# Value projections with 512 moving columns in a decoder trunk's two mixers

## The chip, the core and the metric

The kernel runs on one core of a Trainium2 chip. The metric is the device time of one execution in microseconds (us); the time before is 1752.04, the median of 3 runs that lie between 1751.99 and 1752.09. Engines are named as in the profile: PE (TensorE, matmuls; PEld its weight loads), DVE (VectorE), ACT (ScalarE), POOL (GpSimd), SP (SyncE, which issues most DMA transfers).

## What is computed

A decoder trunk over 512 tokens with 1024 features, in float32: two layers, each a feed-forward block (half step), a mixer, and another feed-forward block (half step), each behind an RMS norm. The mixer of layer 0 is a gated linear attention, that of layer 1 a stick-breaking attention, called the softmax mixer here. Cut to the mixers:

```python
# layer 0: gated linear attention, 4 heads, keys of 128, values of 256
proj = h @ w_in                       # q 512, k 512, v 1024, g 1024, gate rank 16
q, k, v, g, gk_lr = split(proj)
log_a = log_sigmoid(gk_lr @ w_gk2 + b_gk) / 16
...                                   # decayed causal attention of each head: o
o = rmsnorm(o, o_norm) * silu(g)
y = o @ w_out

# layer 1: stick-breaking attention, 16 heads of 64
q, k, v = split(h @ w_in)             # 1024 each
z = q @ k.T / 8                       # strictly causal
w = exp(log_sigmoid(z) - reversed_cumsum(softplus(z)))
y = (w @ v) @ w_out
```

The feed-forward blocks are SwiGLU with 2816 hidden features.

## The kernel before

Every large product is taken in three matmuls: each float32 operand is split into a high part (rounded to fp32r, by an ACT cast) and a low part (the difference, by DVE), and high x high, high x low and low x high are summed in PSUM. For a weight block of 128 x 1024 the cast is line 152 (`wh`) and the difference line 153 (`wl`). Four pairs of such weight buffers exist (`bufs=4`), and two for the raw blocks as they arrive from memory (`raw`, `bufs=2`).

The projections of all phases stand in one queue, `Feed`. An entry has units (weight blocks to be cast) and a body, a generator that emits its matmuls in half-steps. `Feed.start` (lines 160 to 178) begins an entry: it casts the units of up to three entries as long as no more than four weight buffers are taken, and loads the raw blocks of up to six. The mixers' own work, head by head, draws from this queue: `step` takes two half-steps, `halves` single ones. A scheduler then orders the instructions of each engine by its own estimates; engines run their instructions in that order.

Two kinds of entries matter here. `feat` (line 218) has the weights stationary and 512 tokens moving, 24 matmuls with 512 columns in four half-steps; queries, keys and gates are made so. `tok` (line 238) has the tokens stationary, 128 at a time, and 256 weight columns moving: 4 token tiles x 8 blocks of 128 features x 3 = 96 matmuls with 256 columns in eight half-steps, in the PSUM tile `ps_t`. Values are made so, 256 columns an entry, two weight buffers each, and copied out by `evac_v` (lines 1069 and 1425).

Linear attention (`GLA`) queues 8 `feat` entries for queries and keys, then four `tok` entries (all values), then 8 `feat` entries for gates (lines 1042 to 1048). Its run (line 1350) goes over four heads. For each, `levels` prepares scores (`e`, `ps_S`), and `output` of the head before it makes decayed keys (`kd`, transposed by PE into `ps_kd`), states (`st`, `ps_s`) and outputs (`ps_o`, `ps_on`), with a `step` between the pieces (lines 1373 to 1397).

The softmax mixer (`SB`) queues pairs of `feat` entries (`pair(p)`: query and key of heads 2p and 2p+1) and four `tok` entries (`vals`) among them (lines 1421 and 1422). Its run (line 1559) takes 12 half-steps ahead of the heads (4 at line 1583, 8 at line 1587), and then 17 rounds. Round s emits head s's logits (`ps_z`), sigmoids on ACT, scans (`l`, line 1509) and products (`r`, line 1517) on DVE, and head s-1's transposes of `r` (`ps_T`, line 1531), copies (`wt`, line 1534) and, after every second head, the product with the values (`ps_oT`) and its split (`oh`, `ol`). The list `steps` (line 1589) says how many half-steps are drawn in each round. Each finished projection is scaled into `n` and split for the logits (`mq`, `kh`, `kl`, lines 1430 to 1471), at once before the heads, later at set points of a round.

Of the kernel before, what the change touches and what calls it, by code (L numbers as in the profile page):

```python
# [14 lines left out]
AF = mybir.ActivationFunctionType  # L15
# [3 lines left out]
P = 128  # L19
T = 512  # L20
D = 1024
KD = D // P
FF = 2816
NT = T // P
# [6 lines left out]
def turns(t):  # L31

    return t.rearrange("p (two n) -> p n two", two=2)


def flat(ps):

    return ps.rearrange("p (n two) -> p two n", two=2)


def pair(t):

    return t.rearrange("p (two n) -> p two n", two=2)
# [3 lines left out]
def decoder(ctx: ExitStack, tc: tile.TileContext, a: dict, out: bass.AP):  # L47
# [66 lines left out]
    class Entry:  # L114
# [4 lines left out]
        def __init__(self, units, body):  # L119
            self.units, self.body, self.W, self.views = units, body, None, None  # L120
            self.v = None
            self.open, self.sums_behind, self.casts_behind = True, None, None
            self.half = False

        def view(self):

# [5 lines left out]
        def split(self, after=None):  # L132
            if self.W is None:
                self.W = []
                for r, (_, _, n, m) in zip(self.view(), self.units):
# [20 lines left out]
    class Feed:  # L156
# [3 lines left out]
        def start(self):  # L160
            i = self.pos
            self.pos += 1
            used, v = 0, self.q[i].v or {}
            for e in self.q[i : i + 3]:
                if not e.open or e.v is not None and "copied" not in e.v:
                    break
                used += sum(n * m >= 1024 for _, _, n, m in e.units)
                if used > 4:
                    break
                e.split(v.get("summed") if e.half else None)  # L170
            for e in self.q[i : i + 4]:
                if e.open:
                    e.view()
            for e in self.q[i : i + 6]:
                for u in e.units:
                    u[0].load()
            e = self.q[i]
            return e.body(e.W)

        def step(self, n=1, end=None):  # L180
            self.halves(2 * n, end)
# [31 lines left out]
    feed = Feed()  # L213
# [813 lines left out]
    class GLA:  # L1027
        def __init__(self, w_in, w_gk2, b_gk, og, w_out, nxt):
            self.w_in, self.w_gk2, self.b_gk, self.og = w_in, w_gk2, b_gk, og
            self.defer = []  # L1030
            self.q, self.k, self.b, self.v = [None] * 4, [None] * 4, [None] * 4, []
            self.gn, self.on, self.hs = [None] * KD, [None] * KD, []
            chunks = [Chunk(cols(w_in, c * 256, 256), KD, 256) for c in range(4)]

            def qk(h):
                feat(chunks[h // 2], h % 2, lambda ps: self.evac_q(h, ps), "a", self.defer if h < 2 else None)

            def kk(h):
# [29 lines left out]

        def evac_v(self, c, i, ps):
            nc.scalar.activation(  # L1070
                pair(self.v[i][:, c * 256 : c * 256 + 256]), flat(ps), AF.Copy, scale=st["r4"][:, i : i + 1]
            )

        def evac_g(self, j, ps):
# [275 lines left out]
        def run(self):  # L1350
            with ExitStack() as es:
# [51 lines left out]
    class SB:  # L1403
# [5 lines left out]
        def __init__(self, w_in, w_out, nxt):  # L1409
# [6 lines left out]
                    feat(ch, 0, lambda ps, evac=evac: evac(p, ps), "a", d)  # L1416

            def vals(c):
                tok(w_in, 2 * D + c * 256, lambda i, ps: self.evac_v(c, i, ps), "z" if c == 0 else "a")

            pair(0), vals(0), pair(1), pair(2), vals(1), pair(3), pair(4), pair(5)
            vals(2), pair(6), pair(7), vals(3)
            back(w_out, 0, KD, self.hs, 1.0, nxt, late=2, tags=("a", "a", "z", "z", "z", "t", "t", "o"))

        def evac_v(self, c, i, ps):
            nc.scalar.activation(
                pair(self.v[i][:, c * 256 : c * 256 + 256]), flat(ps), AF.Copy, scale=st["r4"][:, i : i + 1]
            )

        def evac_q(self, p, ps):  # L1430
# [128 lines left out]
        def run(self):  # L1559
            with ExitStack() as es:  # L1560
# [421 lines left out]
```

## Time and profile before

| | |
|---|---|
| median of 3 runs | 1752.04 us |
| the profiled execution | 1752.18 us |
| its span, first to last instruction | 1750.2 us |
| DMA, mean over the span | 110 GB/s |
| linear attention, about | 340 to 550 us of the span |
| softmax mixer, about | 1193 to 1400 us of the span |

The span is what the profile covers; the rest of an execution's time lies around it. A group of instructions is given with its count, its busy time, the mean of one in ns, and the idle time of its engine just ahead of it with what ended that. Matmul durations overlap, and their ends are modelled; starts are recorded. Idle time of an engine that nobody waits for costs nothing.

### The profile page before, as it was taken

To read this page: it belongs to the slowest core of one execution; us is meant where nothing else is said; L and a number is where in the kernel's file an instruction comes from. 1 tells how busy PE (TensorE), PEld (TensorE's weight loads), DVE (VectorE), ACT (ScalarE), POOL (GpSimd) and SP (SyncE) were. 2 spreads that over 40 slices of the span, in tenths; PEclk is the share of its full clock that TensorE was granted. 3 is DMA by queue.
4 is the path that set the end of the run, shared out by engine and by line. 5 is a ranking of instruction groups with operands and counts; after the bars stand their busy time and mean duration, and the time that the engine had idled before them with its cause. 6 is when DMAs were issued, how large, how long until landed. Compare 5 with 4: busy or idle time off the path is not lost.

```text
span 1750.2 us, 31332 instructions
## 1 busy us (share of the span) xinstructions
PE 1740.0 (99%) x12698; PEld 1628.1 (93%) x12698; DVE 1507.0 (86%) x2490; ACT 1026.3 (59%) x1832; POOL 55.8 (3%) x85
## 2 busy tenths in 40 slices
PE   9999999999999999999999999999999999999998
PEld 8999999889888899999989999999888889999997
DVE  8999798786888989889799988977999679998886
ACT  7556555554665565555665555555666655565555
POOL 0000000200000000000000000010000000000000
PEclk9999999999999999999999999999999999999999
DMA  5533434412223443444334334343212234434441
GB/s 169 157 109 121 127 116 139 120 55 75 72 75 119 112 129 112 118 129 125 105 125 127 115 118 124 121 111 108 75 59 73 73 97 133 123 107 123 119 140 60
DMA packets 186244, 193.11 MB, mean 110 GB/s; under 512 B 4786, under 2 KB 170980, under 8 KB 186100
## 3 DMA queue, kind: packets, MB, share of 16 engines
q1 hardware_dynamic: 177760, 175.91, 32.3%
q0 software_dynamic: 8096, 14.92, 4.7%
q8 instruction: 99, 1.62, 0.4%
q14 instruction: 45, 0.37, 0.1%
q10 hardware_dynamic: 244, 0.29, 0.0%
HBM read 175.11 MB, written 2.10 MB: 101 GB/s over the span
## 4 chain that ended last, share of the span: by engine, by line
PE 95%; DVE 4%; ACT 1%; issue 0%; DVEq 0%
PE ps_w L779 22%; PE ps_f L80 16%; PE ps_d L80 16%; PE ps_q L779 11%; PE ps_z L779 6%; PE ps_w L412 5%; PE ps_t L80 5%; PE ps_b L80 4%; PE ps_q L412 2%; PE ps_z L412 1%; PE ps_z L1484 1%; PE ps_oT L1546 1%; PE ps_T L1531 1%; PE ps_bt L80 1%; PE ps_S L80 1%; PE ps_o L80 1%
## 5 line engine op out<-in xcount | busy, mean ns | idle before, releaser
L153 DVE TENSOR_TENSOR wl<-raw,wh 128x1024 fp32r<-128x1024 f32 x241 | 255.4, 1060 | 40.5 <-ACT wh L152 39.6
L152 ACT CAST wh<-raw 128x1024 fp32r<-128x1024 f32 x241 | 222.1, 922 | 81.2 <-PE ps_f L80 34.3
L153 DVE TENSOR_TENSOR wl<-s,wh 128x1024 fp32r<-128x1024 f32 x160 | 195.3, 1221 | 66.2 <-ACT wh L152 65.3
L779 PE MATMUL ps_w<-th,wh 128*128 128x256 f32 x864 | 238.8, 276 | 0.0
L779 PE MATMUL ps_w<-tl,wh 128*128 128x256 f32 x864 | 237.6, 275 | 0.0
L779 PE MATMUL ps_w<-th,wl 128*128 128x256 f32 x864 | 237.6, 275 | 0.0
L152 ACT CAST wh<-s 128x1024 fp32r<-128x1024 f32 x160 | 168.7, 1054 | 6.0 <-DVE s L765 6.0
L779 PEld LDWEIGHTS ps_w<-th,wh 128*128 128x128 f32 x864 | 165.8, 192 | 0.5 <-ACT ps_z L807 0.2
L80 PE MATMUL ps_f<-xh,wh 128*128 128x512 f32 x432 | 166.0, 385 | 0.0
L779 PEld LDWEIGHTS ps_w<-tl,wh 128*128 128x128 f32 x864 | 165.9, 192 | 0.0
L779 PEld LDWEIGHTS ps_w<-th,wl 128*128 128x128 f32 x864 | 165.9, 192 | 0.0
L80 PE MATMUL ps_f<-xh,wl 128*128 128x512 f32 x432 | 164.0, 380 | 0.5 <-DVE wl L153 0.5
L80 PE MATMUL ps_f<-xl,wh 128*128 128x512 f32 x432 | 163.8, 379 | 0.0
L80 PE MATMUL ps_d<-hh,wh 128*128 128x512 f32 x416 | 157.8, 379 | 0.0
L80 PE MATMUL ps_d<-hl,wh 128*128 128x512 f32 x416 | 157.7, 379 | 0.0
L80 PE MATMUL ps_d<-hh,wl 128*128 128x512 f32 x416 | 157.7, 379 | 0.0
L153 DVE TENSOR_TENSOR wl<-rawd,wh 128x1024 fp32r<-128x1024 f32 (+1 forms) x100 | 96.2, 962 | 8.6 <-ACT wh L152 8.6
L807 ACT COPY ps_z<-ps_w 128x256 f32<-128x256 f32 x72 | 26.1, 362 | 117.9 <-PE ps_w L779 117.7
L363 POOL DMA_DIRECT2D x<-d x53 | 46.0, 912 | 1525.9 <-ACT d L362 1108.1
L80 PEld LDWEIGHTS ps_f<-xh,wl 128*128 128x128 f32 x432 | 81.8, 189 | 11.4 <-DVE wl L153 0.9
L80 PEld LDWEIGHTS ps_f<-xl,wh 128*128 128x128 f32 x432 | 81.7, 189 | 11.5
L80 PEld LDWEIGHTS ps_f<-xh,wh 128*128 128x128 f32 x432 | 81.7, 189 | 10.7
(355 smaller groups left out, 5355.8 us busy)
## 6 DMA issues: line engine op xcount, KB each, us to landing
raw<-in_ffn_w_gate_dram SPq DMA_DIRECT2D x43, 1024.0 KB, 5.5
raw<-in_ffn_w_up_dram SPq DMA_DIRECT2D x43, 1024.0 KB, 5.4
rawd<-in_ffn_w_down_dram SPq DMA_DIRECT2D x84, 512.0 KB, 3.8
x<-d POOLq DMA_DIRECT2D x53, 256.0 KB, 4.4
raw<-in_gla_w_in_dram SPq DMA_DIRECT2D x12, 1024.0 KB, 5.3
raw<-in_sb_w_in_dram SPq DMA_DIRECT2D x16, 512.0 KB, 3.7
raw<-in_gla_w_out_dram SPq DMA_DIRECT2D x4, 1024.0 KB, 5.0
raw<-in_sb_w_in_dram SPq DMA_DIRECT2D x4, 1024.0 KB, 5.1
```

Of the source, the lines that this page charges most:

```text
L80: st["pe"] = nc.tensor.matmul(ps, l, r, start=first, stop=last).ins
L152: nc.scalar.copy(h[:, k], part)
L153: nc.vector.tensor_tensor(out=l[:, k], in0=part, in1=h[:, k].bitcast(F32), op=ALU.subtract)
L363: nc.gpsimd.dma_start(xs[k], d, accum_op=ALU.add)
L412: st["pe"] = nc.tensor.matmul(ps, l_, r_, start=first and c + n == 0, stop=c == 1 and n == 2, skip_group_check=True).ins
L779: st["pe"] = nc.tensor.matmul(o, l_, r_, start=first and j + n == 0, stop=j == 3 and n == 2, skip_group_check=True).ins
L807: v["copied"] = nc.scalar.copy(z, w).ins
L1484: nc.tensor.matmul(o_, l_, r_, start=first, stop=last, skip_group_check=True)
L1531: nc.tensor.transpose(ps[:, c0 : c0 + P], ys[yb][:, yc + j * P : yc + (j + 1) * P], ident)
L1546: nc.tensor.matmul(po[e * 64 : e * 64 + 64, j * P : T], self.v[j][:, c : c + 64], self.wt[p, e][bk][:, c0 : c0 + n], start=j == 0, stop=j ...
```

## The change

Values are made 512 columns at a time by a new kind of entry, `tok_wide`: 4 token tiles x 8 x 3 = 96 matmuls with 512 columns, in 16 half-steps, each token tile in a PSUM bank of its own. Its weights come as two loads of 512 rows x 512 columns, in four units of 256 rows, so it holds all four weight buffers. Since no entry behind it can then be cast ahead, its units are cast one at a time (`split` with a limit) as buffers come free: up to that count when an entry before it starts, and in its last token tile, `one_more` may cast one more unit of the next two entries after each pair of features. Near such an entry, `loads` keeps no more than two raw blocks in flight.

In linear attention two wide entries take the place of the four narrow ones, one ahead of gates 0 to 3 and one ahead of gates 4 to 7, and the first head draws one more step. In the softmax mixer one wide entry (values 0 to 511) takes the place of `vals(0)` and `vals(1)`; `vals(2)` and `vals(3)` stay narrow. The half-steps ahead of its heads go from 12 to 20, those of its first five rounds from 6 each to 5, 5, 4, 4, 4.

```diff
+    def tok_wide(w, c0, evac, tags):
+        chs = [
+            Chunk(w[u * 4 * P : u * 4 * P + 4 * P, c0 : c0 + T].rearrange("(k p) c -> p k c", p=P), 4, T)
+            for u in range(2)
+        ]
+        def body(W):
+            for i in range(NT):
+                ps = psum("ps_t", tags[i])
+                s = slice(i * P, (i + 1) * P)
+                for k in range(KD):
+                    wh, wl = W[k // 2]
+                    mh, ml = turns(wh[:, k % 2]), turns(wl[:, k % 2])
+                    mm(ps, st["h"][k][:, s], mh, k == 0, False)
+                    mm(ps, st["h"][k][:, s], ml, False, False)
+                    mm(ps, st["l"][k][:, s], mh, False, k == KD - 1)
+                    if k == KD - 1:
+                        evac(i, ps)
+                    if k % 2:
+                        if i == NT - 1:
+                            feed.one_more()
+                        yield
+        feed.q.append(Entry([(ch, (lambda t, u=u: t[:, u : u + 2]), 2, T) for ch in chs for u in (0, 2)], body))
+        feed.q[-1].singly = True
...
             for e in self.q[i : i + 3]:
...
-                used += sum(n * m >= 1024 for _, _, n, m in e.units)
+                before, used = used, used + sum(n * m >= 1024 for _, _, n, m in e.units)
                 if used > 4:
+                    if e.singly:
+                        e.split(limit=4 - before)
                     break
...
+        def one_more(self):
+            for e in self.q[self.pos : self.pos + 2]:
+                n = len(e.W or ())
+                if n < len(e.units):
+                    e.split(limit=n + 1)
+                    self.loads()
+                    return
...
             for c in range(4):
-                tok(w_in, 1024 + c * 256, lambda i, ps, c=c: self.evac_v(c, i, ps), "a")
-            for c in range(4):
+                if c % 2 == 0:
+                    tok_wide(w_in, 1024 + c * 256, lambda i, ps, c=c: self.evac_v(c * 256, i, ps), "aaaa")
                 ch = Chunk(cols(w_in, 2048 + c * 256, 256), KD, 256)
...
-                        if prev is not None and n == 4:
+                        if n == 4:
                             self.step()
...
-            pair(0), vals(0), pair(1), pair(2), vals(1), pair(3), pair(4), pair(5)
+            pair(0), wide(0), pair(1), pair(2), pair(3), pair(4), pair(5)
             vals(2), pair(6), pair(7), vals(3)
...
-                feed.step(4)
-
-                steps = [6] * 5 + [5] * 10 + [4] * 2
+                feed.step(8)
+
+                steps = [5] * 2 + [4] * 3 + [5] * 10 + [4] * 2
```

Where instructions move, the order of an engine shows it. The first place is SP's queue at linear attention: which blocks of its input weights are loaded one after the other, ahead of the output weights and the next feed-forward block. Before:

```order
L108 DMA raw<-in_gla_w_in_dram 128x8x256 x2
L108 DMA rawd<-in_ffn_w_down_dram 128x4x256 x3
L108 DMA raw<-in_gla_w_in_dram 128x8x256 x10
L108 DMA raw<-in_gla_w_out_dram 128x4x512 x4
L108 DMA raw<-in_ffn_w_gate_dram 128x8x256
L108 DMA raw<-in_ffn_w_up_dram 128x8x256
```

Now:

```order
L108 DMA raw<-in_gla_w_in_dram 128x8x256 x2
L108 DMA rawd<-in_ffn_w_down_dram 128x4x256 x3
L108 DMA raw<-in_gla_w_in_dram 128x8x256 x2
L108 DMA raw<-in_gla_w_in_dram 128x4x512 x2
L108 DMA raw<-in_gla_w_in_dram 128x8x256 x2
L108 DMA raw<-in_gla_w_in_dram 128x4x512 x2
L108 DMA raw<-in_gla_w_in_dram 128x8x256 x2
L108 DMA raw<-in_gla_w_out_dram 128x4x512 x4
```

Four of the blocks have become 512 columns wide and half as deep, in two pairs, each pair ahead of two blocks of gates.

The second place is DVE's queue at the last head of linear attention, from the low part of the squared output of head 2 (`sl`, which the matmul `ps_on` takes) to head 3's decayed keys. Before:

```order
L1305 TENSOR_TENSOR sl<-osq,sh 128x512
L1196 COPY_PREDICATED S<-lvl,ps_S 128x8x32
L153 TENSOR_TENSOR wl<-raw,wh 128x1024
L1196 COPY_PREDICATED S<-lvl,ps_S 128x16x16
L1076 TENSOR_TENSOR gn<-ps_f,R 128x512
L1196 COPY_PREDICATED S<-lvl,ps_S 128x32x8
L1311 TENSOR_SCALAR vv<-ps_on 128x512
L1196 COPY_PREDICATED S<-lvl,ps_S 128x64x4
L1241 TENSOR_TENSOR kd<-b 128x384
L153 TENSOR_TENSOR wl<-raw,wh 128x1024
L1082 SCALAR_TENSOR_TENSOR sg<-gn,sg 128x512
L1248 TENSOR_TENSOR kd<-kd,k 128x384
```

Now:

```order
L1367 TENSOR_TENSOR sl<-osq,sh 128x512
L1138 TENSOR_TENSOR gn<-ps_f,R 128x512
L159 TENSOR_TENSOR wl<-raw,wh 128x1024
L1144 SCALAR_TENSOR_TENSOR sg<-gn,sg 128x512
L1373 TENSOR_SCALAR vv<-ps_on 128x512
L1303 TENSOR_TENSOR kd<-b 128x384
L1148 TENSOR_TENSOR gn<-gn,sg 128x512
L1310 TENSOR_TENSOR kd<-kd,k 128x384
```

The copies of scores now stand ahead of `sl`; one weight difference has left the stretch, and a gate's product stands between the two steps of `kd`.

The third place is DVE's queue in the softmax mixer, from head 2's first scan (`l`, 384 columns) to its last product (`r`, 511 columns). Before:

```order
L1509 SCALAR_TENSOR_TENSOR l_14120<-l_14120,own 128x384
L1465 TENSOR_TENSOR kl<-n,kh 64x512
L1517 TENSOR_TENSOR r_14126<-r_14126,l_14120 128x383
L1466 CAST kl<-kl 64x512
L1464 CAST kh<-n 64x512
L1465 TENSOR_TENSOR kl<-n,kh 64x512
L1509 SCALAR_TENSOR_TENSOR l_14121<-l_14121,own 128x256
L1466 CAST kl<-kl 64x512
L1509 SCALAR_TENSOR_TENSOR l_14121<-l_14121,own 128x128
L1509 SCALAR_TENSOR_TENSOR l_14119<-l_14119,own 128x512
L1517 TENSOR_TENSOR r_14130<-r_14130,l_14121 128x383
L1517 TENSOR_TENSOR r_14122<-r_14122,l_14119 128x511
```

Now:

```order
L1574 SCALAR_TENSOR_TENSOR l_13918<-l_13918,own 128x384
L1582 TENSOR_TENSOR r_13924<-r_13924,l_13918 128x383
L1506 TENSOR_TENSOR mq<-n,mq 64x512 x2
L1574 SCALAR_TENSOR_TENSOR l_13919<-l_13919,own 128x256
L1574 SCALAR_TENSOR_TENSOR l_13919<-l_13919,own 128x128
L1574 SCALAR_TENSOR_TENSOR l_13917<-l_13917,own 128x512
L1582 TENSOR_TENSOR r_13928<-r_13928,l_13919 128x383
L1582 TENSOR_TENSOR r_13920<-r_13920,l_13917 128x511
```

Head 2's scans now stand among the split of pair 2's query instead of that of its key: the projections come to the heads later.

More of the change, by code (lines that the diff above doesn't have):

```diff
@@ L122, in __init__, with waiting @@
             self.open, self.sums_behind, self.casts_behind = True, None, None
-            self.half = False
+            self.half = self.singly = False
+        def waiting(self):
+            return [u[0] for u in self.units[len(self.W or ()) :] if u[0].t is not None]
         def view(self):
@@ L130, in view, with split @@
             return self.views
-        def split(self, after=None):
+        def split(self, after=None, limit=None):
             if self.W is None:
                 self.W = []
-                for r, (_, _, n, m) in zip(self.view(), self.units):
+            if len(self.W) < len(self.units):
+                todo = list(zip(self.view(), self.units))[len(self.W) : limit]
+                for r, (_, _, n, m) in todo:
                     self.W.append(self.parts(r, n, m, after or self.casts_behind))
@@ L166, in start, with loads @@
                     break
-                used += sum(n * m >= 1024 for _, _, n, m in e.units)
+                before, used = used, used + sum(n * m >= 1024 for _, _, n, m in e.units)
                 if used > 4:
+                    if e.singly:
+                        e.split(limit=4 - before)
                     break
                 e.split(v.get("summed") if e.half else None)
-            for e in self.q[i : i + 4]:
+            self.loads()
+            e = self.q[i]
+            return e.body(e.W)
+        def loads(self):
+            i = self.pos - 1
+            near = self.q[i : i + 6]
+            if any(e.singly for e in near):
+                live = set()
+                for e in near:
+                    live.update(id(ch) for ch in e.waiting())
+                for e in near:
+                    for u in e.units[len(e.W or ()) :]:
+                        if u[0].t is None:
+                            if len(live) == 2:
+                                return
+                            live.add(id(u[0]))
+                            u[0].load()
+                return
+            for e in near[0:4]:
                 if e.open:
                     e.view()
-            for e in self.q[i : i + 6]:
+            for e in near:
                 for u in e.units:
                     u[0].load()
-            e = self.q[i]
-            return e.body(e.W)
+        def one_more(self):
[3 more added lines that the diff above has]
+                    e.split(limit=n + 1)
+                    self.loads()
+                    return
         def step(self, n=1, end=None):
@@ L1070, in evac_v @@
             nc.scalar.activation(
-                pair(self.v[i][:, c * 256 : c * 256 + 256]), flat(ps), AF.Copy, scale=st["r4"][:, i : i + 1]
+                pair(self.v[i][:, c : c + ps.shape[1]]), flat(ps), AF.Copy, scale=st["r4"][:, i : i + 1]
             )
```

6 lines of the change are left out of this document (4 added, 2 removed).

## The prediction

> **What bounds the kernel now.** The page comes first: how much of the span each engine is busy, and which engine the chain that ended last runs through.
>
> ```profile
> span 1750.2 us, 31332 instructions
> PE 1740.0 (99%) x12698; PEld 1628.1 (93%) x12698; DVE 1507.0 (86%) x2490; ACT 1026.3 (59%) x1832; POOL 55.8 (3%) x85
> PE 95%; DVE 4%; ACT 1%; issue 0%; DVEq 0%
> core 0: 1750.2 us, clock 0.999
> ```
>
> PE is busy 99% of the span, 95% of the chain is PE, and its clock is granted in full (0.999). So the time is the sum of matmul starts plus the few places where PE stands still. What one matmul costs is not its duration, since these overlap, but the distance between starts. The chain of work shows that in its merged pieces (start, length, count):
>
> ```profile
> 389.29 8.04 PE ps_t L80 x72
> 1193.15 10.36 PE ps_f L80 x48
> ```
>
> 72 matmuls with 256 moving columns (values, ps_t) take 8.04 us, **111.7 ns** each; 48 with 512 columns take 10.36 us, **215.8 ns** each. Two narrow ones cost 223.3 ns, one wide one 215.8 ns: 7.5 ns are in play per pair.
>
> The second limit differs by stage. The table by stretches (start:end, length, busy PE, PEld, DVE, ACT) for linear attention once the gates run, and for the softmax mixer while heads and projections alternate:
>
> ```profile
> 448.00:484.00 36.00, 35.52 (x286) 31.87 (x287) 33.32 (x64) 25.01 (x42) 0.00 (x0) 1.00 0.16 54
> 1284.00:1304.70 20.70, 20.70 (x124) 17.43 (x123) 19.94 (x30) 15.35 (x30) 0.00 (x0) 1.00 0.18 52
> 1304.70:1325.00 20.30, 20.30 (x156) 18.10 (x155) 19.20 (x28) 13.49 (x29) 0.00 (x0) 1.00 0.20 60
> ```
>
> In the softmax mixer DVE is busy 19.94 of 20.70 us beside a PE that never stops: there DVE is all but the bound too, and what moves PE work out of that stretch takes away DVE's time.
>
> **The change, part by part.** *Wider matmuls.* Linear attention had 4 value chunks x 4 token tiles x 8 k x 3 = 384 narrow matmuls; now 192 wide ones. The softmax mixer had as many, and half become 96 wide ones. 288 pairs x 7.5 ns = **-2.2 us** (linear attention -1.4, softmax mixer -0.7). The weight loads halve too and stay hidden: PEld is busy less than PE in every row above.
>
> The pitch row has a counterpart. The Trainium skill ("TensorE: Matmul & The Clock Gate", section "Back-to-back issue gap") puts the warm distance at N/2.4 + 2.5 ns. By that a pair would save 2.5 ns, an estimate of 0.7 us in all, and the sum at the end would be 1753.1; the row for 512 columns agrees with it (215.8 against 215.8), the row for 256 does not (111.7 against 109.2), and the row decides.
>
> *Evacuation.* One ACT copy of 512 columns takes the place of two of 256:
>
> ```profile
> L1070 ACT ACTIVATE v<-ps_t,r x16: 455/467/478, 396.8 to 442.8; 128x256 f32<-128x256 f32 x16
> raw<-in_gla_w_in_dram SPq DMA_DIRECT2D x12, 1024.0 KB, 5.3
> raw<-in_sb_w_in_dram SPq DMA_DIRECT2D x16, 512.0 KB, 3.7
> ```
>
> Two of them are 0.93 us, so one wide one lies between 0.47 and 0.93 us, on an engine with room, while a token tile of PE takes 24 x 0.216 = 5.2 us and the next tile has another PSUM bank: costed at nothing. *Loads.* Bytes and their number stay; SP's queue issues two 1024 KB blocks ahead of each wide entry, 5.3 us each, while the entry itself lasts 4 x 5.2 = 20.7 us. That hides them: nothing. Were it gone, a late block would cost up to its 5.3 us once.
>
> *Handover at a wide entry's end.* It holds all four weight buffers, so the next gate block is cast only while the last token tile runs. The first buffer is free after 6 of its 24 matmuls, 3.9 us before the end; cast and difference have to fit in.
>
> ```profile
> L153 DVE TENSOR_TENSOR wl<-raw,wh 128x1024 fp32r<-128x1024 f32 x11 | 13.4, 1222 | 0.6 <-ACT wh L152 0.4
> L152 ACT CAST wh<-raw 128x1024 fp32r<-128x1024 f32 x8 | 8.4, 1054 | 3.0 <-PE ps_f L80 2.9
> ```
>
> 1.05 + 1.22 = 2.3 us leave 1.6 us. I take nothing; if ACT and DVE were each one such instruction behind, 2.3 us late, each of the three handovers would cost 0.7 us.
>
> *End of linear attention.* One more feed step early on leaves half a gate entry (12 matmuls, 2.6 us) instead of a whole one between ps_on of head 2 and the transposes of kd of head 3. Before:
>
> ```profile
> 497.16 0.38 PE L80 MATMUL ps_on<-sl,one 128*128 128x512 f32 x1
> 499.14 0.68 DVE L1311 TENSOR_SCALAR vv<-ps_on 128x512 f32<-128x512 f32 x1
> 500.08 0.54 DVE L1241 TENSOR_TENSOR kd<-b 128x384 f32<-128x384 f32 x1
> 502.28 0.55 DVE L1248 TENSOR_TENSOR kd<-kd,k 128x384 f32<-128x384 f32 x1
> 503.35 0.68 DVE L1086 TENSOR_TENSOR gn<-gn,sg 128x512 f32<-128x512 f32 x1
> 502.97 0.52 PE L1259 MATMUL ps_kd<-ident,kd 128*128 128x128 f32 x3
> ```
>
> kd is ready at 502.83, 0.14 us ahead of PE. In the new DVE order vv, kd, gn and kd*k follow ps_on: 0.68 + 0.54 + 0.68 + 0.55 = 2.45 us against a cover of 2.6 + 0.2. So the cost is 0 if DVE is free there, 2.6 us if kd is as late as now; what stands queued ahead (wl, sg) makes me take **+0.5**.
>
> *Softmax mixer.* All eight half-steps of values 256 to 511 (12 matmuls each, 12 x 111.7 ns = 1.34 us) leave the heads and stand ahead of them. Up to head 5 the same projections are done, but PE has 8 x 1.34 = 10.7 us less to do between head 0's first logits and the point where it wants head 7's weights. What DVE had there:
>
> ```profile
> 1221.20:1306.80 85.60, 77.38 (x114) 1.00 0.26 75
> 1253.81 0.69 DVE L1556 TENSOR_TENSOR ol<-ps_oT,oh 128x512 fp32r<-128x512 f32 x1 [1.06 <-ACT oh L1555]
> 1263.32 0.69 DVE L1432 SCALAR_TENSOR_TENSOR n<-ps_f,R 128x512 f32<-128x512 f32 x1 [1.71 <-PE ps_f L80]
> 1264.41 1.23 DVE L153 TENSOR_TENSOR wl<-raw,wh 128x1024 fp32r<-128x1024 f32 x1 [0.41 <-ACT wh L152]
> 1276.54 0.69 DVE L1556 TENSOR_TENSOR ol<-ps_oT,oh 128x512 fp32r<-128x512 f32 x1 [2.37 <-ACT oh L1555]
> 1306.11 0.69 DVE L1517 TENSOR_TENSOR r<-r,l 128x511 f32<-128x511 f32 x1
> 1308.66 0.60 PE L1531 MATMUL ps_T<-ident,r 128*128 128x128 f32 x4
> ```
>
> Head 7's last product ends at 1306.80, and PE starts the transposes that take it at 1308.66 (the fourth of them reads it, some 0.2 us in): slack 2.1 us. DVE gains what it no longer does there: the 11 weight differences of the row quoted above (it is for this stretch) become 9 (two values blocks are gone, two projections' are done ahead, two more are drawn in), 2 x 1.22 = 2.4 us. It can gain its long idle times, 1.06 + 1.71 + 0.41 + 2.37 = 5.55 us, if none is left. 2.1 + 2.4 + 5.55 = 10.05 against 10.7: **even a DVE that never waits makes PE wait 0.7 us**. If none of the idle time goes, it is 6.2 us. The nearer end is the low one, because a DVE that is behind finds its inputs there; the order of heads 2 to 4 shows where it gets tight first (their steps shrink from 6 half-steps to 4). ACT then copies late, being queued behind casts that wait for DVE:
>
> ```profile
> L1534 ACT COPY wt<-ps_T 128x512 f32<-128x512 f32 x13 | 7.5, 597 | 0.6 <-PE ps_T L1531 0.5
> ```
>
> One such copy, 0.6 us, in PE's way: 0.7 + 0.6, **+1.3 us**.
>
> *Sum*, against the profiled execution's own 1752.18 us: -2.2 + 0.5 + 1.3 = -0.4, that is 1751.8; the median of the runs, 1752.04, lies 0.14 lower, so **1751.6 us**.
>
> **The rivals.**
>
> *All hidden.* DVE closes its gaps and the slack of other heads absorbs the rest. For it: in the softmax mixer PE's only wait that the profile names is this one,
>
> ```profile
> PE ps_b L80 <- ACT w L1426: 0.2, 1, 0.2
> ```
>
> so DVE, at 96%, has never held it up. Against: the sum of 10.05 against 10.7. 1752.04 - 2.2 = 1749.8.
>
> *DVE becomes the bound in the heads (slower).* The waits of DVE for oh come from the queue's order, not from lack of time: if all 5.55 us stay, PE waits 6.2 us, with the 0.5 us at the end of linear attention 1752.04 - 2.2 + 6.2 + 0.5 = 1756.5. It makes the kernel slower once more than 1.0 us of idle time is left (2.2 - 0.5 - 0.7); it would pass 0.2% from 4.5 us on. Against: two of the four gaps (1.71 and 0.41) wait for PE or a cast that would be long done. Half of them left is 1753.8.
>
> *A matmul carries a large fixed cost.* The durations, read as costs, say so:
>
> ```profile
> L80 PE MATMUL ps_t<-wl,xh 128*128 128x256 f32 x256 | 70.4, 275 | 0.0
> L80 PE MATMUL ps_b<-ol,wh 128*128 128x512 f32 x128 | 48.2, 380 | 0.0
> ```
>
> 2 x 275 - 380 = 170 ns a pair, 49 us in all, 1703 us. The starts above speak against it: those durations overlap. The Trainium skill ("TensorEngine Tiling (Array Packing)", section "Instruction Overhead") states some 60 cycles for each matmul; at the 2.4 GHz of its page on TensorE that is an estimate of 25 ns, 7.2 us in all, 1744.8. The 7.5 ns of the rows deny that as well.
>
> *It doesn't do what it says*: no way for that is seen; the order of the changed kernel has 128x512 rows in both mixers.
>
> **How the numbers follow.** The forecast (1750.8 to 1752.8): 0.40. All hidden (1749 to 1750.8): 0.28. Part of DVE's idle time stays, or a handover is late (1752.8 to 1755.5): 0.15. DVE the bound (over 1755.5): 0.13. Fixed cost, and any gain of its kind below 1748.5: 0.04. The range takes in all hidden, with 0.3 us below it, and the part of the idle time up to 0.2%: **1749.5 to 1755.5**. A measurement of this kernel tells about 0.2%, 3.5 us, from no change; so faster by more than that (below 1748.5) 0.04, within 0.83, slower (above 1755.5) 0.13.
>
> **What would show it.** In the changed profile ps_t runs at 215 to 217 ns from start to start, 192 + 96 matmuls. PE waits for DVE before ps_z or ps_T of heads 2 to 7 of the softmax mixer, 1 to 3 us together, and DVE's gaps for oh are gone between heads 0 and 7. Before kd of head 3 in linear attention PE stands 0 to 1 us. The forecast is wrong if ps_t's pitch is under 214 or over 218 ns, if PE waits for a cast (wh) or a load at the first matmuls of a gate entry, or if DVE's gaps stay and PE waits over 4 us.

## The result and the profile after

| | before | changed |
|---|---|---|
| median of 6 runs each | 1752.01 us | 1758.87 us |
| range of these runs | 1751.50 to 1752.37 | 1757.57 to 1760.62 |
| profiled execution | 1752.18 | 1759.04 |

The ratio is 1.0040, with a 95% interval of 1.0027 to 1.0053: 6.9 us slower, clear of no change by that interval, where 0.4 us faster had been forecast and 1755.5 us was the upper end of the range. These runs also lie further apart, 3.0 us against 0.9.

The page of the changed kernel, the lines that answer to those of before (and its clock):

```profile
span 1757.1 us, 30737 instructions
PE 1741.4 (99%) x12410; PEld 1619.5 (92%) x12410; DVE 1507.9 (86%) x2490; ACT 1025.9 (58%) x1820; POOL 55.8 (3%) x85
PE 85%; DVE 11%; ACT 2%; issue 1%; DMA 1%; DVEq 0%; ACTq 0%
core 0: 1757.1 us, clock 0.998
```

288 matmuls fewer, the same DVE work, and the chain that ended last now runs through DVE for 11% of the span instead of 4%. The pitch is what was forecast; a piece of the chain in linear attention has 36 wide matmuls in 7.77 us, 215.8 ns each:

```profile
391.83 7.77 PE ps_t L80 x36
```

Where the time is, comes out when the starts of the same PE instructions are compared between the two traces (medians over all matched ones of a stretch; the changed kernel later by):

| stretch of the span (before) | later by |
|---|---|
| 300 to 343, ahead of linear attention | -0.04 us |
| 520 to 690, behind its heads | +1.32 us |
| 705 to 1200, feed-forward blocks | +2.79 us |
| 1335 to 1380, behind the mixer's heads | +6.98 us |
| 1400 to 1700 | +6.85 us |

So there are three places, not two: linear attention +1.4, **a feed-forward block between 690 and 705 us, which the change doesn't touch, +1.5**, and the softmax mixer +4.2. What PE waited for in the three (view of waits, by stretch: total, times, longest):

```profile
PE ps_kd L1321 <- DVE kd L1310: 2.0, 3, 1.2
PE ps_f L80 <- DVE wl L159: 0.8, 1, 0.8
PE ps_b L80 <- ACT oh L1398: 0.2, 1, 0.2
```

```profile
DVE s L826 <- DMA raw<-in_ffn_w_gate_dram: 1.8, 1, 1.8
...
PE ps_w L841 <- ACT ps_z L869: 0.7, 1, 0.7
```

```profile
PE ps_T L1596 <- ACT wt L1599: 1.8, 1, 1.8
PE ps_T L1596 <- DVE r L1582: 0.5, 1, 0.5
PE ps_b L80 <- ACT w L1491: 0.2, 1, 0.2
```

In the softmax mixer PE's wait of 1.8 us is followed by something that no wait shows. The table by stretches (length, PE, PEld, DVE, ACT, POOL, then PEclk, DMA share, GB/s):

```profile
1296.00:1300.00 4.00, 2.18 (x12) 0.98 (x12) 3.94 (x6) 3.31 (x6) 0.00 (x0) 1.00 0.12 31
1300.00:1303.40 3.40, 3.40 (x16) 2.14 (x13) 3.24 (x7) 0.90 (x3) 0.00 (x0) 0.50 0.40 120
1303.40:1306.00 2.60, 2.60 (x15) 2.33 (x15) 2.60 (x4) 2.18 (x6) 0.00 (x0) 0.99 0.00 0
```

Behind the wait PE's clock is granted at **one half for 3.4 us**, the only time between the start, where it reaches full at 6.4 us, and the last 3 us. The page's slices of 44 us don't show it; the mean of 0.998 does, barely.

### The profile page after: what moved, and what is told of

Same layout as the page of the kernel before. It is cut to its first block, busy times and chain, and to the rows that moved or that the text cites. A ratio compares the mean times of both kernels' runs of the same rounds, so it can differ in the third digit from the quotient of the medians.

```text
span 1757.1 us, 30737 instructions
## 1 busy us (share of the span) xinstructions
PE 1741.4 (99%) x12410; PEld 1619.5 (92%) x12410; DVE 1507.9 (86%) x2490; ACT 1025.9 (58%) x1820; POOL 55.8 (3%) x85
## 4 chain that ended last, share of the span: by engine, by line
PE 85%; DVE 11%; ACT 2%; issue 1%; DMA 1%; DVEq 0%; ACTq 0%
PE ps_w L841 21%; PE ps_d L80 15%; PE ps_f L80 12%; PE ps_q L841 10%; PE ps_z L841 5%; PE ps_w L474 5%; PE ps_b L80 4%; PE ps_t L80 4%; PE ps_q L474 2%; DVE wl L159 2%; PE ps_z L474 1%; DVE l L1574 1%; PE ps_bt L80 1%; PE ps_oT L1611 1%; PE ps_z L1549 1%
```

## The experiments

The first theory was that both losses come from moved work: gates' DVE work ahead of `kd`, projections taken away from DVE's heads. Its rival was the wide entry itself. The first four runs take the mixers apart, and then the order from the width. Each is timed against the kernel before on the same chip.

**Each mixer alone.** In the first run the softmax mixer is as before, in the second linear attention is.

```diff
 # e1_gla_only
-            pair(0), wide(0), pair(1), pair(2), pair(3), pair(4), pair(5)
+            pair(0), vals(0), pair(1), pair(2), vals(1), pair(3), pair(4), pair(5)
...
-                feed.step(8)
+                feed.step(4)
-                steps = [5] * 2 + [4] * 3 + [5] * 10 + [4] * 2
+                steps = [6] * 5 + [5] * 10 + [4] * 2
 # e2_sb_only
-                if c % 2 == 0:
-                    tok_wide(w_in, 1024 + c * 256, lambda i, ps, c=c: self.evac_v(c * 256, i, ps), "aaaa")
+                tok(w_in, 1024 + c * 256, lambda i, ps, c=c: self.evac_v(c * 256, i, ps), "a")
+            for c in range(4):
...
-                        if n == 4:
+                        if prev is not None and n == 4:
```

> Linear attention as changed (wide values, gate entries between them, the extra step), softmax mixer as before. Theory: the two losses are apart, and linear attention's is PE waiting for DVE (kd of heads 2 and 3 and one weight difference), 2.3 us more than before: 1752.0 + 2.3 = 1754.3 (1753.8 to 1754.9). Rival: the two mixers' losses depend on each other through the loads: then this one lies outside of 1753.3 to 1755.4.

> Softmax mixer as changed (one wide entry ahead of the heads, new steps), linear attention as before. Theory: 1752.0 + 4.5 = 1756.5 (1755.7 to 1757.5), DVE with no idle time over 0.2 us between its first scan and head 7's last product. Rival: most of the loss belongs to linear attention, and this one is under 1754.5.

1754.57 us (ratio 1.0014, 1.0005 to 1.0022) and 1757.04 us (1.0027, 1.0016 to 1.0038). +2.5 and +5.0 make 7.5 against 6.9: within their intervals the two losses add up. In the first one's trace the feed-forward block at 693 us loses its 1.6 us as well, so that belongs to linear attention's change. Both theories' ranges held, the first one's by luck in part: its 2.3 us of waits were there, but less the pitch they leave 1.4 behind linear attention, and the other 1.6 are that block. In the second one's trace DVE has no idle time over 0.15 us between its first scan and head 7's last product, as the theory said.

**The order without the width.** The entries stand as in the changed kernel, but the values are narrow.

```diff
 # e3_gla_moved
-                    tok_wide(w_in, 1024 + c * 256, lambda i, ps, c=c: self.evac_v(c * 256, i, ps), "aaaa")
+                    for d in (c, c + 1):
+                        tok(w_in, 1024 + d * 256, lambda i, ps, d=d: self.evac_v(d * 256, i, ps), "a")
 # e4_sb_moved
-            pair(0), wide(0), pair(1), pair(2), pair(3), pair(4), pair(5)
+            pair(0), vals(0), vals(1), pair(1), pair(2), pair(3), pair(4), pair(5)
```

> Linear attention in the new order (values 0 to 511, four gate entries, values 512 to 1023, four gate entries, the extra step) but with the values 256 columns wide, softmax mixer as before. Theory: the loss comes from the gates' DVE work that now stands ahead of kd, whatever the width: the same waits as in the changed kernel and the 1.0 to 1.4 us of pitch more, 1755.0 to 1755.8. Rival: the loss comes from the wide entry, which needs four blocks of weights at once and hands them over all at its end: then this one stays within 1751.5 to 1752.8.

> Softmax mixer in the new order (values 0 to 511 ahead of the heads, new steps) but with all values 256 columns wide, linear attention as before. Theory: taking eight half-steps out of the heads makes DVE the bound there, whatever the width: +4.5 + 0.7 = +5.2, 1757.2 (1756 to 1758.2). Rival: the wide entry is at fault (DVE stands idle for 10.6 us ahead of the heads while it waits for casts of the following blocks, so that it starts the heads late): then this one is under 1754.5.

1752.85 us (1.0004, 0.9995 to 1.0013) and 1753.97 us (1.0012, 1.0003 to 1.0021). **Both expectations of the theory fell.** The order costs 0.8 and 1.9 us, and width, which should save 1.4 and 0.7, costs 1.7 and 3.1 on top. Part of the 3.1 is a different mix of runs: the seven runs of the order alone with a mean clock of 0.999 or more have a median of 1753.4 us, the three lowest of the softmax mixer alone, its profile among them, lie at 1755.5 to 1755.7, which leaves 2.2. In linear attention the rival's range was missed by a hair, in the softmax mixer the rival was right.

**Why the wide entry starts DVE late.** The rival's reading: the wide entry holds four weight buffers, and behind it the queue has only two raw buffers. ACT and the first key evacuation on DVE in the run with the softmax mixer alone, at the wide entry's end, and PE's first logits:

```profile
1222.10 1.05 ACT L158 CAST wh<-raw 128x1024 fp32r<-128x1024 f32 x1 [0.61 <-PE ps_t L80]
1223.44 1.06 ACT L158 CAST wh<-raw 128x1024 fp32r<-128x1024 f32 x1 [0.29 <-PE ps_t L80]
1225.99 0.69 ACT L1491 ACTIVATE w<-ps_t,r 128x512 f32<-128x512 f32 x1 [1.49 <-PE ps_t L80]
1229.67 1.04 ACT L158 CAST wh<-raw 128x1024 fp32r<-128x1024 f32 x1 [2.99 <-DMA raw<-in_sb_w_in_dram]
1231.19 1.05 ACT L158 CAST wh<-raw 128x1024 fp32r<-128x1024 f32 x1 [0.48 <-DMA raw<-in_sb_w_in_dram]
```

```profile
1230.96 0.33 PE L1549 MATMUL ps_z<-kh,mq 128*128 128x384 f32 x1
```

```profile
1241.74 0.83 DVE L1516 TENSOR_TENSOR n<-ps_f,R 128x512 f32<-128x512 f32 x1
```

The next two blocks are cast when the last token tile frees weight buffers (1222.10, 1223.44). Only these casts free the raw buffers, only then the loads of the following two blocks start, and their casts wait for them (2.99 us). Their differences fall on DVE when the heads have begun, and DVE, without idle time from then on, doesn't make it up: it evacuates the first key 10.8 us behind the first logits, against 8.8 before (1221.04 and 1229.88). The next run gives two chunks a place of their own, in the pool of the heads' outputs, which is empty at that time.

```diff
 # e5_sb_raw, against e2_sb_only; loads() counts such chunks apart from the two raw buffers
+                if self.own is not None:
+                    return self.halves()
...
+        def halves(self):
+            n = self.n // 2
+            self.t = tuple(
+                st["own"].tile([P, T], F32, tag=tag, name="rawx").rearrange("p (k c) -> p k c", c=self.m)
+                for tag in ("oh", "ol")
+            )
...
+                    if p == 1:
+                        ch.own = True
```

> As the run with the softmax mixer alone changed (1757.0, 1755.5 where the clock is not halved), but the two weight chunks of the entry behind the wide one land in buffers of their own (four loads of 256 KB in place of two of 512 KB, two casts and two differences of 512 columns a block), so that the next two chunks need not wait for them. Theory: DVE enters the heads 2.4 us later than with narrow values, because ACT's casts wait for loads that only start when the wide entry has freed its buffers; with the loads early DVE's first scan comes within 1.5 us of PE's first logits (now 3.05) and PE's waits of 1.5 us at heads 2 and 3 go: 1753.0 to 1755.0. Rival: DVE's total in the heads is what counts, not its start: 1756.3 or more.

1753.38 us (1.0012, 1.0003 to 1.0021), 3.7 less, within the theory's range; three of its eleven runs still lie at 1757.2 to 1757.7. The first key's evacuation:

```profile
1238.89 0.83 DVE L1536 TENSOR_TENSOR n<-ps_f,R 128x512 f32<-128x512 f32 x1
```

That is 8.4 us behind the first logits (1230.49), 2.4 less, and PE's waits at heads 2 and 3 are gone. The two casts that waited for loads (1229.67 and 1231.19 above) start at 1224.26 and 1226.10 here and wait for none. With the order alone changed the key is 8.4 us behind as well (1233.45 and 1241.84): the late start belongs to the wide entry. DVE's first scan, the landmark that was named, misled: with another order on DVE it came later, not earlier.

**DVE's sum.** PE's wait for ACT's copy is still there, 1.8 us. ACT runs in order, and ahead of that copy (`wt`) stands a cast that waits for DVE's evacuation (`n`). ACT, and the transposes of PE that wait, in the run with the buffers:

```profile
1291.79 1.26 ACT L1563 CAST kh<-n 64x512 fp32r<-64x512 f32 x2 [2.39 <-DVE n L1536]
1293.07 1.07 ACT L1619 COPY wt<-ps_T 128x512 f32<-128x512 f32 x2
```

```profile
1293.71 0.44 PE L1616 MATMUL ps_T<-ident,r 128*128 128x128 f32 x2 [1.82 <-ACT wt L1619]
```

Two kinds of runs take work off DVE in the heads: the weight differences to POOL, or one of two key casts to ACT.

```diff
 # e6_sb_pool, against e2_sb_only; for the entries behind the wide one
-                nc.vector.tensor_tensor(out=l[:, k], in0=part, in1=h[:, k].bitcast(F32), op=ALU.subtract)
+                eng = nc.gpsimd if self.on_pool else nc.vector
+                eng.tensor_tensor(out=l[:, k], in0=part, in1=h[:, k].bitcast(F32), op=ALU.subtract)
 # e10_sb_raw_act, against e5_sb_raw; e12_sb_act is the same against e2_sb_only
-                    nc.vector.tensor_copy(m[oth], t[own])
+                    cast(m[oth], t[own])
```

> As the run with the softmax mixer alone changed, but the weight differences behind the wide entry (14 blocks, some 10 of them in the heads before PE's longest wait) go to POOL, which is idle there. Theory: DVE, busy without a gap, is what PE and ACT wait for; 10 x 1.22 us less for it is more than the 4.5 us that PE waits, so the waits of PE in heads 2 to 6 go, with them the spell at half clock and the spread between runs: 1751.3 to 1752.5. Rival: ACT or the loads hold PE: 1755.5 or more, with the wait for ACT's copy still above 1 us.

1769.56 us (1.0100, 1.0087 to 1.0114). That lies in the rival's open range, but it is no test of either, since POOL's differences slow DVE's own instructions and take 2.4 to 2.8 us each themselves. The same group in the run with the softmax mixer alone, and here (busy time, mean ns):

```profile
L1530 DVE TENSOR_TENSOR kl<-n,kh 64x512 fp32r<-64x512 f32 x10 | 6.8, 683 | 0.2
```

```profile
L1535 DVE TENSOR_TENSOR kl<-n,kh 64x512 fp32r<-64x512 f32 x10 | 10.9, 1094 | 0.2
```

DVE is slower by 60% in that group on average, and not evenly: the six of the ten that met no difference of POOL took 684 ns as before, the four that did 1709 ns. PE's waits for `r` and for ACT's copy grow to 7.1 and 3.3 us.

> As the run with the softmax mixer alone changed and buffers of their own for two weight chunks (1753.4; 1752.4 where the clock is not halved), but one of the casts of each key half, 64x512, moves from DVE (0.42 us) to ACT (0.63 us): some 10 in the heads before PE's longest wait, 4.2 us less for DVE and 6.3 us more for ACT, whose share there is about 70%. Theory: DVE's sum is what PE waits for behind ACT's copy (1.8 us); the wait goes below 0.5 us, no spell at half clock is left, the runs lie close together: 1750.9 to 1752.0. Rival: ACT's own queue is what holds the copy: the wait grows, 1754 or more.

> As the run with the softmax mixer alone changed (1757.0; 1755.6 in its profile, where the clock is not halved), with a key cast of each half moved from DVE to ACT, but without the buffers of their own. Theory: the late start (2.4 us) and DVE's sum (4.2 us less now) are one account, so either relief alone takes away most of the waits, and this one more than the buffers did: 1751.8 to 1753.2. Rival: they are two accounts; the waits at heads 2 and 3 (1.5 us) come from the late start and stay, only ACT's copy (1.8 us) comes in time: 1753.5 to 1755.

1751.90 us (1.0002, 0.9993 to 1.0011) with the buffers, 1754.39 us (1.0015, 1.0007 to 1.0024) without. PE's waits in the mixer with the buffers:

```profile
PE ps_T L1616 <- ACT wt L1619: 0.5, 1, 0.5
```

and without:

```profile
PE ps_T L1596 <- ACT wt L1599: 1.9, 2, 1.6
PE ps_T L1596 <- DVE r L1582: 0.6, 2, 0.5
```

With both reliefs the mixer is back at the time of before, within the theory's range, though the runs are not as close together as expected (1751.18 to 1753.64). With the cast alone the 1.6 us stay, and the theory that one account is as good as the other fell. The rival's number came out, and not as it said: the copy it expected in time is the one that is still late. In the traces the mixer costs 3.5 us with neither relief, 0.9 with the buffers, 2.5 with the cast, -0.4 with both: the two reliefs nearly add up, so late loads and DVE's sum are two costs. What the moved cast would give the kernel of before was not run.

**The feed-forward block at 693 us.** In the changed kernel the load of a gate weight there took 6.6 us where the median of its kind is 5.4. Its end, by stretches, and the packets by queue in one microsecond of it (packets, MB, share of 16 engines):

```profile
685.00:686.00 1.00, 1.00 (x11) 1.00 (x10) 0.60 (x1) 1.00 (x3) 0.00 (x0) 1.00 0.27 90
686.00:687.40 1.40, 1.40 (x15) 1.40 (x14) 0.00 (x0) 0.60 (x3) 0.00 (x0) 1.00 0.04 15
```

```profile
q1 hardware_dynamic: 355, 0.36, 103.1%
q8 instruction: 1, 0.02, 6.0%
```

The load is all but done at 686 us and trickles at 15 GB/s for 1.4 us more. In its middle, at 683.5, one packet of **instructions** went through the same 16 DMA engines. q1's 0.36 MB in that microsecond are 22 GB/s for each engine, so the trickle looks like the one engine that had to serve both; the trace doesn't name the engine of a packet. Before, that fetch came at 687.4, behind the load, which had landed by 685:

```profile
q8 instruction: 1, 0.02, 5.7%
```

In this stretch one such packet comes every 11 to 17 us. With 192 matmuls fewer on PE this one comes at 683.5 in place of 687.4 us, though PE's work there is 1.3 us later. Putting 64 back should move them out of the load:

```diff
 # e7_gla_split, against e1_gla_only; e9_gla_first_split: the same against e8_gla_wide_first
-                    mm(ps, st["h"][k][:, s], ml, False, False)
+                    for half in range(2):
+                        c = slice(half * 256, half * 256 + 256)
+                        mm(ps[:, c], st["h"][k][:, s], ml[:, half * P : half * P + P], False, False)
 # e8_gla_wide_first, against e1_gla_only
-                if c % 2 == 0:
-                    tok_wide(w_in, 1024 + c * 256, lambda i, ps, c=c: self.evac_v(c * 256, i, ps), "aaaa")
+            for c in range(0, 4, 2):
+                tok_wide(w_in, 1024 + c * 256, lambda i, ps, c=c: self.evac_v(c * 256, i, ps), "aaaa")
+            for c in range(4):
...
-                        if n == 4:
+                        if prev is not None and n == 4:
```

> As the run with linear attention alone changed (1754.6), but one of the three wide matmuls of each step is two of 256 columns: 64 instructions more on PE, and 64 x 7.5 ns = 0.5 us. In that run's trace a fetch of instructions (16 KB, one about every 15 us in this stretch) falls into the load of a gate weight at 683 us, the load's last packets trickle at 22 GB/s and it takes 6.7 in place of 5.3 us; PE waits 0.7 us at 693 and is 1.5 us later behind it. Theory: the 192 matmuls that the wide form saves moved the fetches by half of their spacing; 64 of them put back move the fetch out of the load: -1.5 + 0.5, 1753.6 (1753.2 to 1754.0). Rival: the load is slow because the stage ahead ended late: 1754.9 to 1755.3, with the wait at 693 still there.

1754.99 us (1.0016, 1.0007 to 1.0025), the rival's number, and yet not for the rival's reason: the wait at 693 is gone from this trace, and nothing is lost between 690 and 705. The fetch now lies at 691.1 us in the next load, which takes 7.4 us and delays nothing. But linear attention loses 3.6 us instead of 1.4, because the last wait for `kd` grew to 2.1 us, and PE's clock was halved behind it:

```profile
505.80:509.00 3.20, 3.20 (x9) 2.48 (x9) 3.04 (x5) 2.41 (x6) 0.00 (x0) 0.50 0.20 15
```

Why that wait grew with 64 more instructions was not followed up. The clean test came with the next two runs.

**The gates behind both wide entries.** The chain of work at the wait for `kd` of head 1 in the changed kernel (the expectations call it head 2) is DVE alone, and the gates' instructions (`sg`, `gn`) stand in it, ahead of `kd`, with the output products (`on`, `ol`) that take them:

```profile
434.48 0.60 DVE sg L1144
435.08 0.60 DVE on L1395
435.68 0.34 DVE e L1240
436.01 0.60 DVE gn L1148
436.62 0.47 DVE kd L1303
437.08 0.60 DVE on L1395
437.69 0.60 DVE ol L1399
438.29 0.47 DVE kd L1310
```

> Linear attention with both wide entries ahead of all gate entries and without the extra step, as the narrow values stood before; softmax mixer as before. Theory: the waits for kd of heads 2 and 3 come from the gates' DVE work, which the changed order puts ahead of them; in the old order they go: -1.0 by the pitch, up to +0.8 for one handover, and +1.5 where the fetch of instructions falls into the load at 683 us as in the run with linear attention alone changed: 1751.0 without the fetch, 1752.5 with it. Rival: the wide entry itself costs 2.7 us (it frees all its weights at its end): 1754 or more.

> As the run with both wide entries ahead of the gates (1751.87), with one of its three wide matmuls as two of 256 columns (64 instructions more on PE, 0.5 us). In that run linear attention ended 1.1 us earlier than before, and 1.25 us were lost at 693 us, where a fetch of instructions at 681.5 lay in the load of a gate weight (678.0 to 684.7 us). Theory: 64 instructions more bring the fetch some 5 us earlier, out of the load; the wait at 693 goes: 1751.87 - 1.25 + 0.5 = 1751.1 (1750.8 to 1751.4). Rival: the load is slow for another reason: 1752.3, with PE's wait of 0.6 us still there.

1751.87 us (1.0000, 0.9991 to 1.0009) and 1751.13 us (0.9997, 0.9988 to 1.0006). Counted from its start, linear attention ends 1.1 us earlier than before in the first trace and 0.8 in the second, which pays for 64 instructions more; its waits are those of before. In the first one the fetch lies at 681.5 us, inside the load, and takes the gain back (+1.25); in the second fetches lie at 674.8 and 686.5, on either side of the load, and the gain stays. The theory's figure for the first with the fetch, 1752.5, was 0.6 too high; that for the second, 1751.1, was met. By their medians alone the two runs could hardly be told apart; the traces tell them apart. All 14 traces settle it: that load took 6.6 to 6.7 us in the three in which a fetch lay in it (the changed kernel, linear attention alone, the first run here), and these lost 1.2 to 1.6 us between 690 and 705; in the other eleven it took 5.2 to 5.5 us, and they lost 0.25 or less. PE's waits from 340 to 720 us in the first:

```profile
PE ps_w L841 <- ACT ps_z L869: 0.6, 1, 0.6
PE ps_kd L1321 <- DVE kd L1310: 0.5, 1, 0.5
PE ps_S L80 <- DVE st L1343: 0.3, 1, 0.3
PE ps_b L80 <- DVE wl L159: 0.2, 1, 0.2
```

and in the second:

```profile
PE ps_kd L1323 <- DVE kd L1312: 0.5, 1, 0.5
PE ps_S L80 <- DVE st L1345: 0.2, 1, 0.2
PE ps_b L80 <- DVE wl L159: 0.2, 1, 0.2
```

**Both mended.** Linear attention as in the last run, the softmax mixer as in the run with buffers and cast.

```diff
 # e11_both, the parts of e9_gla_first_split and e10_sb_raw_act
-    def tok_wide(w, c0, evac, tags):
+    def tok_wide(w, c0, evac, tags, pieces=1):
...
-                tok_wide(w_in, 1024 + c * 256, lambda i, ps, c=c: self.evac_v(c * 256, i, ps), "aaaa")
+                tok_wide(w_in, 1024 + c * 256, lambda i, ps, c=c: self.evac_v(c * 256, i, ps), "aaaa", 2)
```

> Both mixers with their losses mended: linear attention with both wide entries ahead of the gates and one wide matmul of three in two pieces (1751.1), softmax mixer with the wide entry, buffers of their own for two weight chunks and a key cast moved from DVE to ACT (1751.9). Theory: the two add up, 1751.8 - 0.7 + 0.1 = 1751.2, and less where the softmax mixer's own profile (0.4 us shorter than before) is the typical one: 1750.3 to 1751.4. Rival: the fetches of instructions fall elsewhere and another load is caught: above 1752.

1751.04 us (0.9996, 0.9986 to 1.0005), against 1752.00 for the kernel before in the same job, within the theory's range. The median is 1.0 us lower, but the interval holds no change: a version without the loss, and not one that can be called faster.

## Why the prediction was wrong

*The pitch was right, its sum slightly high.* 215.8 ns it is. With both wide entries ahead of the gates linear attention gained 1.1 us, not 1.4; the softmax mixer's 0.7 could not be seen apart.

*The step that failed in the softmax mixer is "Loads": "That hides them: nothing."* It looked only at the two blocks of the wide entry itself. What is late are not its own blocks and not the next two but the two after these, which have no raw buffer until the wide entry hands over. By the traces the mixer costs 3.5 us with the late loads and 0.9 without (each profile at full clock), 2.6 us for a term that stood at nothing. The bound written beside it, "up to its 5.3 us once", would have held it; the range didn't use that bound.

*DVE's account was right.* Between its first scan and head 7's last product DVE took 84.65 us before and 76.35 in the run with the softmax mixer alone, 8.3 us less; the forecast was 2.4 + 5.55 = 8.0. The first scan before, and the first scan and that product in the run:

```profile
1222.15 0.96 DVE L1509 TENSOR_TENSOR_SCAN l<-l,own 128x384 f32<-128x384 f32 x1 [0.22 <-ACT l L656]
```

```profile
1234.01 0.95 DVE L1574 TENSOR_TENSOR_SCAN l<-l,own 128x384 f32<-128x384 f32 x1
1309.67 0.69 DVE L1582 TENSOR_TENSOR r<-r,l 128x511 f32<-128x511 f32 x1
```

DVE's gaps for `oh` are gone, as said. With the late loads away the mixer costs +0.9, where the forecast was -0.7 + 1.3 = +0.6. The 0.6 us for "one such copy" was too small: the copy is 1.8 us late, and what it waits for is a cast that itself waits for DVE. So PE was held at DVE's rate by way of ACT, and moving casts of 0.42 us off DVE took that wait to 0.5 us, with the buffers in place.

*The rival "DVE becomes the bound" gave about the right size (1756.5) by the wrong mechanism*: it had DVE's idle time stay, and DVE had none left.

*The end of linear attention was mis-sized.* Forecast +0.5 for `kd` of head 3; it waited 1.2 us there, 0.6 at head 1, which the prediction didn't look at, and 0.8 for a weight difference at the second wide entry's handover, which stood at nothing: the cast was in time, but DVE was busy with outputs. The 0.7 written beside it was about right, for one handover. A wait of 0.5 us for `kd` of head 2, there before, shrank to 0.2. The added waits all go when the gates stay behind the values. Narrow values in the new order still lost 0.8 us; in that trace the 0.6 at head 1 is there, but `kd` of head 3 waits 0.3 and no handover waits, so the rest takes both the order and the wide entry. The run without these waits also left out the extra step, and what that step alone does was not tried. The step that failed is to have priced one moved half entry at one place, when four gate entries had moved ahead of three heads' `kd` on a queue that runs in order.

*Two terms were missing.* Behind linear attention the moved fetch of instructions costs 1.5 us in a block that the diff doesn't touch. And a wait of 1.8 us can cost PE half its clock for 3.4 us. In the profiles that is 0.7 us (4.2 against 3.5 in the softmax mixer); with the order alone changed it may be more, since its four runs at a mean clock of 0.998 lie at 1755.0 to 1757.1 us and the other seven have a median of 1753.4.

Together, from the profiles: linear attention 1.4, fetch 1.5, late loads 2.6, the rest of the mixer 0.9, the clock 0.7, behind it -0.1: 7.0 of 6.9 us.

## What to carry over

When a tuned kernel's entry is made larger, ask of each buffer that it holds what the *next but one* entry needs it for; the cost comes where the buffers change hands, on the engine that has no spare time. Work that moves ahead in an in-order queue is priced at every consumer that it now stands before, and a late instruction on one engine reaches PE by way of another's queue. And below 0.2% a change of instruction count can move time in stages that it doesn't touch: compare the starts of the same instructions in both traces before a cause is looked for in the diff.

## What the hardware showed beyond this

*The clock gate takes less than it seemed.* The trace's clock record changes only on a grid of 3.413 us (full clock for 1293.651 us, that is 379 steps, then half for 3.413). In each trace PE's idle time within one step of that grid can be laid beside what followed:

| trace | PE idle | most of it within one step | half clock behind it |
|---|---|---|---|
| changed kernel | 1.82 us at 1296.7 | 1.82 | 3.41 us |
| order alone, softmax mixer | 1.81 at 1294.9 | 1.81 | 3.41 us |
| 64 matmuls split | 2.10 at 502.5 | 2.10 | 3.41 us |
| POOL | 2.23 at 1242.4; 3.31 at 1304.6 | 2.23; 2.20 | 6.83 us each |
| POOL | 2.24 at 1275.2 | 1.36 | none |
| softmax mixer alone | 1.82 at 1294.8 | 1.08 | none |
| with own buffers | 1.82 at 1291.9 | 1.51 | none |
| changed kernel | 1.24 at 502.9 | 1.24 | none |

So the same 1.82 us costs a halved clock or not by where it falls on the grid; from 1.81 us within a step on it did, up to 1.51 it did not. The grid's place differs from run to run, which fits the spread in part. Of the changed kernel's six runs the four with a mean clock of 0.998 are the four slowest, and so are the four of the eleven with the order alone. In the softmax mixer alone, which ran at 1755.5 to 1755.7 three times in seven and above 1757.0 otherwise, only the slowest run shows 0.998, so there the cause of the spread stays open; the late start below is a rival. The Trainium skill ("TensorE: Matmul & The Clock Gate", section "Part 1: The HAM clock gate") has the free-running window of 3.413 us, and these records agree with it; it also puts the fall to half clock behind an idle window of some 3.4 us, and here a little over half of one sufficed.

*The start has a spread too.* The profile of the softmax mixer's order alone is 1.7 us later than before ahead of linear attention already; its clock record goes to full at 10.3 us, that of before at 6.2. In the other twelve traces it goes to full at 3.9 to 6.7 us, and they are within 0.4 us of before there. In one job four runs of the kernel before lie at 1753.2 to 1754.1 us, against its median of 1752.06; their starts are not on record.

*Fetches of instructions share the DMA engines with loads*: 97 to 99 packets of 16 KB in a run, and the load of 1 MB at 683 us that met one took 6.6 us, against a median of 5.4. Not every meeting costs: over the 14 traces, of the loads of gate and up weights with no other weight load beside them, 80 of 228 with such a fetch in their time took over 6 us, and 17 of 621 without one.
